# The planner of a hybrid encoder kernel gets other estimates of the waits of VectorE and GpSimd for their shared SBUF ports

## The chip, the cores and the metric

The kernel runs on one core of a Trainium2 chip. The metric is the device time of one execution in microseconds. TensorE (PE in the profile, its weight loads PEld), VectorE (DVE), ScalarE (ACT), GpSimd (POOL) and the DMA queue of SyncE (SP) each work through a list of instructions of their own, in a fixed order; semaphores tie the lists together.

## The reference: what is computed

Two sequences of 512 and 256 tokens with 1024 channels go through the same two layers. Each layer adds its mixer's output to the scaled input and normalises the sum over the channels:

```python
alpha = (2.0 * DEPTH) ** 0.25
for i in range(DEPTH):              # DEPTH = 2: kind 0, then kind 1
    if kind == 0:   h = _mamba2_mixer(x, ...)
    elif kind == 1: h = _rwkv7_mixer(x, ...)
    x = _layernorm(alpha * x + h, ln_g[i], ln_b[i])
```

The first mixer is a bidirectional Mamba-2 block: a projection to z, x, B, C and dt, a centred convolution of width 5 with a silu, a state-space scan in chunks of 128 tokens forward and backward, a gate with silu(z), an RMS norm in 8 groups, and a projection back. The second is a bidirectional RWKV-7 block: a projection to r, k, v, g and two low-rank inputs, a token shift, a decay and a learning rate for each channel, a delta-rule scan with a 64 x 64 state for each of 16 heads in both directions, a group norm, a bonus term, a gate and a projection back. All of it is float32.

## The kernel before, in words

The 768 tokens of both sequences are treated together. Every large projection is split: a float32 operand is rounded to a `float32r` part (ScalarE, L126, L139) and a rest (VectorE `tensor_sub`, L127, or for two of the eight input blocks GpSimd, L140), and three matmuls (L144 to L146) replace one.

The Mamba stage (about 0 to 620 us) loops over 8 channel groups. For each it projects four blocks, convolves them on VectorE (L236, L238, L244), builds for each of 6 chunks the weighted decay matrix `G` (GpSimd L418, VectorE L413, L419, L420) and the output `yv` (GpSimd L429 and L440, VectorE L441 and L442). The scale `sk` of the skip term is a small VectorE operation on 4 elements for each partition (L428) that reads two small SBUF tiles. The output projection and the layer norm follow until about 740 us.

The RWKV stage (about 840 to 1500 us) loops over 8 blocks of 128 channels. It projects r, k, v, g for a later block, prepares keys and decays in windows of 256 tokens (`p1_front`, `p1_back`: VectorE L880, L900, L906, L916, L919; GpSimd L903, L905, L907, L932, L934), inverts small triangular matrices (`rwkv_inverse`, L954 to L990), and runs the scan in 8 steps a block (`chain_step`: matmuls L1018 and L1040, GpSimd L1054, VectorE L1057, L1066, L1068). `rwkv_final` (L1091 to L1120) normalises the output, on GpSimd except in the last block. `rsqrt` (L100 to L112) is a chain of nine small VectorE operations, used by the RMS norm (`rms`), the key norm (`nk`), the group norm (`ng`) and the layer norm (`ln`). The output projection (L505) and the last layer norm end the program.

The order in which each engine issues its instructions is not that of the source. After the program is built, `arrange` (L1888) makes a model of it, plans it, and pins each engine's order with dependencies from each instruction to the one before it. Tiles and buffers are given out before that and do not depend on the plan. The model has a `cost` for each instruction (`estimate`, L1374), a table of times from one engine to the next (`HANDOVER`, L1248), and a model of TensorE's clock: a period in which too little dense matmul work was done is followed by one at half rate (`TICK`, `WARM`, L1859 on). `schedule` (L1811) builds 12 plans one after another for each of four parameter sets, each with due times from the plan before, and keeps the one with the best modelled time over four modelled runs, three of them with random DMA delays.

For the ports that VectorE and GpSimd share, an instruction may have a `lock`, the part of its cost during which it is taken to hold the ports. `Machine.run` uses it so:

```python
end = t + p.cost[i]
if p.lock[i]:
    other = "Pool" if e == "DVE" else "DVE"
    end = max(end, self.held[other] + p.lock[i])
    self.held[e] = end
```

An instruction with a lock thus cannot end earlier than `lock` after the end of the other engine's last locked instruction: `lock` is what remains to be done once the other engine lets go. In the kernel before, `lock` is `cost - 60` ns for every GpSimd operation but memsets, and for VectorE operations without a PSUM operand if they have more than 16 elements for each partition.

Of the kernel before, what the change touches and what calls it, by code (L numbers as in the profile page):

```python
# [59 lines left out]
class Trunk:  # L60
# [1103 lines left out]
    def run(self):  # L1164
        self.mamba()
        self.rwkv()
# [108 lines left out]
def size(ap, first=1):  # L1275
    return math.prod(int(n) for _, n in ap.ap[first:])


def on_chip(ap):

    (ps, pn), *free = [(int(s), int(n)) for s, n in ap.ap]
    p0, lo = divmod(int(ap.offset), ps) if ps else (0, int(ap.offset))
    bits = 1
    for k, (s, n) in enumerate(free):
        if n == 1 or s == 0:
            continue
        if k == len(free) - 1 and abs(s) > 1:
            s, n = int(math.copysign(1, s)), (n - 1) * abs(s) + 1
        if s < 0:
            lo += s * (n - 1)  # L1290
            s = -s
        cur, have, pos, acc = bits, 1, 0, 0
        while have <= n:
            if n & have:
                acc |= cur << (s * pos)
                pos += have
            cur |= cur << (s * have)
            have *= 2
        bits = acc
    return p0 // 32, (p0 + pn + 31) // 32, bits << lo  # L1300
# [19 lines left out]
def space(t, name):  # L1320
    return str(t._space).endswith(name)


class Program:
# [49 lines left out]
    def estimate(self, i, x, src, dst):  # L1374
        e, op = self.eng[i], x.opcode
        if e == "SP":
            dram = src and dst and any(hasattr(a.tensor, "cap_key") and space(a.tensor, "DRAM") for a in src + dst)
            self.cost[i] = 1.0 if not dst else 560.0 if dram else 400.0
            if dram and len(dst[0].ap) > 2:
                self.cost[i] = 650.0  # L1380
            if dst:
                n = size(dst[0], 0)
                self.dma[i] = n * 4 / 250.0
                self.late[i] = max(0, n / min(run(a) for a in src + dst) - 128) * 2.3
                if any(s == 0 and k > 1 for a in src for s, k in a.ap):
                    self.late[i] += 1100.0
            return
        if e == "PE":
            N, M, K = size(src[0]), size(src[1]), int(src[0].ap[0][1])
            f32 = str(x.ins[0].dtype) == "dt.float32"  # L1390
            up = lambda n: 32 if n <= 32 else 64 if n <= 64 else 128
            rows, cols = (range(*on_chip(a)[:2]) for a in (src[1], dst[0]))
            self.cells[i] = [4 * r + c for r in rows for c in cols]
            if x.is_transpose:
                self.cost[i] = 2 * max(N, M) / 2.4 + 2.5
                self.cols[i] = 2 * N * K / 128
                self.extra[i] = 57.0
                return
            self.mode[i] = up(K), up(M)
            if not f32:  # L1400
                r = self.fast[i] = str(x.ins[0].dtype) == "dt.float32r"
                self.extra[i] = 106.0
                self.cost[i] = (N * 17 / 16 + 16) / 2.4 if r else N / 2.4 + 2.0
                self.cols[i] = N * K / 128
                if N >= 256:
                    self.kind[i] = 2
                    if r and M <= 64:
                        self.mode[i] = FULL
                return
            cyc = 4 * max(N, M)  # L1410
            if M > 64 and N < 64:
                cyc = 1022
            self.cost[i] = cyc / 2.4 + 2.5
            self.cols[i] = (2 if M <= 64 else 4) * N * K / 128
            if M <= 64:
                self.cost[i], self.extra[i] = (114.5, 20.0) if max(K, M) <= 32 else (116.6 if N <= 64 else N * 1.703, 49.0)
                self.leave[i] = 100 + 0.82 * N
                self.kind[i] = 0
            return
        N = max(size(a) for a in src + dst)  # L1420
        rows = on_chip(dst[0])[:2] if hasattr(dst[0].tensor, "_space") and int(dst[0].ap[0][1]) > 1 else (0, 4)
        if rows != (0, 4) and int(dst[0].ap[0][1]) >= 32:
            self.part[i] = rows
        ps = any(space(a.tensor, "PSUM") for a in src + dst if hasattr(a.tensor, "_space"))
        ptr = sum(1 for a in src if size(a) == 1 and N > 1)
        two = len(src) - ptr
        if e == "DVE":
            if op != "TensorScalarPtr":
                c = (66 + N) / 0.96
                if op == "Reciprocal":  # L1430
                    c = 70 + N * 6.4
            elif x.ins and two == 1 and not ps:
                c = 69 + N / 1.92 + 61 * ptr
            else:
                c = (66 + N) / 0.96 + 61 * ptr
            if any(N > 64 and len(a.ap) > 1 and abs(int(a.ap[-1][0])) >= 16 and space(a.tensor, "SBUF") for a in src + dst):
                c += 0.78 * N
            if getattr(x, "is_tensor_tensor_scan", False):
                c = 70 + 2.07 * N
            if not ps and N > 16:  # L1440
                self.lock[i] = c - 60
        elif e == "Activation":
            far = any(N > 64 and len(a.ap) > 1 and abs(int(a.ap[-1][0])) >= 16 for a in src + dst)
            c = 51 + N * (1.9 if far else 0.8333) + (0 if ps else 43) + 93.5 * ptr + (93 if len(dst) > 1 else 0)
        elif op == "Memset":
            c = 35 + 0.8333 * N
        elif op == "TensorScalarPtr":
            c = 130 + N * 0.83 + 90 * ptr
            self.lock[i] = c - 60
        elif two > 1:  # L1450
            c = 185 + 1.6 * N if N < 200 else 222 + 1.75 * N
            self.lock[i] = c - 60
        else:
            c = 130 + 0.9 * N
            self.lock[i] = c - 60
        self.cost[i] = c

    def node(self, pred):
# [472 lines left out]
```

## Time and profile before

| what | before |
| --- | --- |
| time, median of 3 runs | 1620.61 us (1617.91 to 1621.78) |
| profiled execution, own time | 1633.23 us |
| span of the profiled execution | 1631.4 us |
| mean granted TensorE clock | 0.955 |
| instructions | 39329 |
| PE busy | 1516.9 us (93%) |
| VectorE busy | 1342.4 us (82%) |
| ScalarE busy | 858.0 us (53%) |
| GpSimd busy | 709.8 us (44%) |

The profile is one execution. A group's row names the line, the engine, the operation, the tiles it writes and reads, the shape and the count, then the busy time in us, the mean duration of one in ns, and the engine's idle time before the group with what ended it. A row for one line gives the least, the median and the largest duration in ns. The time that an operation waits for the ports is inside its duration, since it has started by then.

### The profile page before, as it was taken

What the parts mean: (1) busy time and instruction counts of PE and PEld (TensorE: products, weight loads), DVE (VectorE), ACT (ScalarE), POOL (GpSimd) and SP (SyncE); (2) the same over time, 40 slices, a digit from 0 to 9 for tenths busy, and PEclk for the clock granted to TensorE, in tenths of its full rate; (3) what the DMA queues carried; (4) which work ended last, traced back from release to release, by engine and by line L of the source; (5) the groups of instructions that cost most, each with busy time, mean ns of one, the idle gap of its engine ahead of it and who ended that gap; (6) DMA issues with size and microseconds to landing.
All of it is one profiled execution on the core that took longest, in us unless ns stands there. A gap on an engine that the chain in (4) does not pass through costs nothing. (4 is left out here: it accounts for less than half of the span.)

```text
span 1631.4 us, 39329 instructions
## 1 busy us (share of the span) xinstructions
PE 1516.9 (93%) x15210; PEld 1287.0 (79%) x15210; DVE 1342.4 (82%) x2947; ACT 858.0 (53%) x1988; POOL 709.8 (44%) x983
## 2 busy tenths in 40 slices
PE   7999999999999899998987899989998989978996
PEld 6878888888889699997766777777777777766876
DVE  6769988898797995668689798889899897887759
ACT  4245454544444452424464758577675747574332
POOL 1158475585483670000162527355464628264210
PEclk9999999999999999999989899989999999986988
DMA  5110211212212044612345234443435242344422
GB/s 171 58 52 21 79 39 59 72 65 72 66 40 72 23 154 122 196 53 104 119 128 157 54 116 118 119 141 104 140 99 159 82 140 83 105 145 135 139 71 85
DMA packets 150315, 161.41 MB, mean 99 GB/s; under 512 B 39632, under 2 KB 106928, under 8 KB 150128
## 3 DMA queue, kind: packets, MB, share of 16 engines
q1 hardware_dynamic: 150128, 158.89, 32.2%
q8 instruction: 120, 1.97, 0.5%
q14 instruction: 67, 0.55, 0.1%
HBM read 121.43 MB, written 40.55 MB: 99 GB/s over the span
## 5 line engine op out<-in xcount | busy, mean ns | idle before, releaser
L144 PE MATMUL pj<-xh,whi 128*128 128x512 f32 (+1 forms) x1056 | 381.6, 361 | 20.4 <-ACT whi L126 11.6
L146 PE MATMUL pj<-xh,wlo 128*128 128x256 f32 (+1 forms) x1056 | 374.8, 355 | 3.9 <-DVE wlo L127 3.9
L145 PE MATMUL pj<-xl,whi 128*128 128x512 f32 (+1 forms) x1056 | 373.7, 354 | 0.9 <-DVE xl L140 0.9
L144 PEld LDWEIGHTS pj<-xh,whi 128*128 128x128 f32 x1056 | 205.2, 194 | 50.9 <-ACT whi L126 13.0
L146 PEld LDWEIGHTS pj<-xh,wlo 128*128 128x128 f32 x1056 | 204.2, 193 | 30.6 <-DVE wlo L127 6.4
L145 PEld LDWEIGHTS pj<-xl,whi 128*128 128x128 f32 x1056 | 204.6, 194 | 25.8 <-issue 2.1
L126 ACT CAST whi<-wraw 128x512 fp32r<-128x512 f32 x213 | 131.1, 620 | 128.2 <-PE pj L145 57.9
L127 DVE TENSOR_TENSOR wlo<-wraw,whi 128x512 fp32r<-128x512 f32 x213 | 156.1, 738 | 40.2 <-ACT whi L126 38.1
L418 POOL TENSOR_SCALAR G<-past,ddt,dt 128x128 f32<-128x128 f32 x192 | 133.6, 708 | 73.7 <-DVE ddt L324 59.0
L144 PE MATMUL po<-whi,xh 128*128 128x256 f32 x528 | 153.0, 290 | 0.6 <-DVE acc L505 0.5
L145 PE MATMUL po<-wlo,xh 128*128 128x256 f32 x528 | 152.9, 290 | 0.0
L146 PE MATMUL po<-whi,xl 128*128 128x256 f32 x528 | 152.2, 288 | 0.0
L238 DVE SCALAR_TENSOR_TENSOR conv<-conv,convw 128x770 f32<-128x770 f32 x128 | 142.2, 1111 | 1.4
L144 PE MATMUL pz<-whi,xh 128*128 128x256 f32 x384 | 114.7, 299 | 0.0
L382 POOL TENSOR_TENSOR xw<-xB,dtws 128x256 f32<-128x256 f32 x64 | 55.7, 877 | 130.7 <-ACT xB L370 115.3
L145 PE MATMUL pz<-wlo,xh 128*128 128x256 f32 x384 | 111.9, 291 | 0.0
L146 PE MATMUL pz<-whi,xl 128*128 128x256 f32 x384 | 110.2, 287 | 0.0
L903 POOL TENSOR_TENSOR G<-EP,Wr 64x256 f32<-64x256 f32 x96 | 85.5, 891 | 49.4 <-DMA Wr<-ind 26.9
L1054 POOL TENSOR_TENSOR ZP<-SV,PC 64x128 f32<-64x128 f32 x128 | 68.4, 543 | 86.2 <-DVE SV L1066 59.8
L144 PEld LDWEIGHTS po<-whi,xh 128*128 128x128 f32 x528 | 101.7, 193 | 2.3 <-DVE acc L505 0.9
L145 PEld LDWEIGHTS po<-wlo,xh 128*128 128x128 f32 x528 | 102.2, 194 | 1.6 <-DVE wlo L127 0.6
L146 PEld LDWEIGHTS po<-whi,xl 128*128 128x128 f32 x528 | 102.0, 193 | 1.2
(289 smaller groups left out, 3831.4 us busy)
## 6 DMA issues: line engine op xcount, KB each, us to landing
wraw<-in_r_w_in SPq DMA_DIRECT2D x72, 256.0 KB, 3.1
Wr<-ind SPq DMA_DIRECT2D x48, 384.0 KB, 3.7
wraw<-in_m_w_xbc SPq DMA_DIRECT2D x64, 256.0 KB, 2.6
wraw<-in_m_w_z SPq DMA_DIRECT2D x32, 256.0 KB, 2.7
wraw<-in_m_w_out SPq DMA_DIRECT2D x32, 256.0 KB, 3.0
ydram<-yst SPq DMA_DIRECT2D x16, 384.0 KB, 4.6
yraw<-ydram SPq DMA_DIRECT2D x24, 256.0 KB, 4.9
ind<-k SPq DMA_DIRECT2D x32, 192.0 KB, 2.8
```

The source lines that it names most:

```text
L126: nc.scalar.copy(hi, raw)
L127: nc.vector.tensor_sub(lo, raw, hi.bitcast(F32))
L144: mm(ps, ah, bh, start=first, stop=False)
L145: mm(ps, ah, bl, start=False, stop=False)
L146: mm(ps, al, bh, start=False, stop=last)
L238: nc.vector.scalar_tensor_tensor(acc, u[:, t : t + n], w[:, b, t : t + 1], acc, op0=ALU.mult, op1=ALU.add)
L382: nc.gpsimd.tensor_tensor(hv(xw), hv(xB[c][:, 0:256]), bc(self.dtws[:, c, z, hs], 2, 64), op=ALU.mult)
L418: nc.gpsimd.tensor_scalar(G[:, h, :], self.past, self.ddt[:, c, i : i + 1], self.dt[:, c, 0, i : i + 1], op0=ALU.mult, op1=ALU.add)
L903: nc.gpsimd.tensor_tensor(G[hr, ps4, h, 0, :], EP[hr, :, 0:C], w4(tok(W[hr, h])), op=ALU.mult)
L1054: nc.gpsimd.tensor_tensor(ZP[HR[h], :, s, :], SV[HR[h], :, s, h, :], bc(pc[s][HR[h]], 2, C), op=ALU.mult)
```

## The change

Only `estimate` is changed, and only `lock`, with one `cost`. For VectorE operations without a PSUM operand the lock becomes `cost - 52`, and operations of 16 elements or fewer get one too. For GpSimd the lock becomes `cost - 95` (operations with scalars from SBUF, `TensorScalarPtr`), `cost - 130` (two tensor inputs) or `cost - 87` (the rest). A GpSimd operation on two tensors whose output is `float32r` costs 115 ns more. The instructions, their operands, the tiles and their places stay as they are; the plan is made anew with these numbers, so the order may differ on every engine and in SyncE's queue.

```diff
-            if not ps and N > 16:
-                self.lock[i] = c - 60
+            if not ps:
+                self.lock[i] = c - 52
...
         elif op == "TensorScalarPtr":
             c = 130 + N * 0.83 + 90 * ptr
-            self.lock[i] = c - 60
+            self.lock[i] = c - 95
         elif two > 1:
             c = 185 + 1.6 * N if N < 200 else 222 + 1.75 * N
-            self.lock[i] = c - 60
+            if str(x.outs[0].dtype) == "dt.float32r":
+                c += 115
+            self.lock[i] = c - 130
         else:
             c = 130 + 0.9 * N
-            self.lock[i] = c - 60
+            self.lock[i] = c - 87
         self.cost[i] = c
```

## The prediction, made before the result was known

> **What bounds the kernel now.** I read the page first, then the busy time by stretches, then who TensorE waited for, then the groups of VectorE and GpSimd in the stretch that has slack. The page:
>
> ```profile
> span 1631.4 us, 39329 instructions
> PE 1516.9 (93%) x15210; PEld 1287.0 (79%) x15210; DVE 1342.4 (82%) x2947; ACT 858.0 (53%) x1988; POOL 709.8 (44%) x983
> ```
>
> TensorE is the bound, with 1631.4 - 1516.9 = 114.5 us idle. The stretches (start and end, length, busy us of PE, PEld, DVE, ACT, POOL with instruction counts, granted clock, DMA share, GB/s) say where; the row of sums is that of six stretches from 20 to 620 us:
>
> ```profile
> sum 600.00, PE 590.50 PEld 510.86 DVE 512.64 ACT 283.13 POOL 334.60; mean PE 98.42 PEld 85.14 DVE 85.44 ACT 47.19 POOL 55.77
> ...
> 840.00:1500.00 660.00, 596.97 (x7939) 475.85 (x7939) 578.22 (x1310) 425.50 (x1047) 327.14 (x491) 0.92 0.41 119
> ...
> 1150.00:1250.00 100.00, 92.27 (x1181) 72.51 (x1180) 91.40 (x220) 62.28 (x154) 49.63 (x72) 0.97 0.44 127
> ...
> 1400.00:1450.00 50.00, 43.76 (x539) 35.11 (x539) 46.10 (x125) 30.73 (x72) 20.03 (x28) 0.89 0.50 147
> 1450.00:1500.00 50.00, 40.45 (x598) 32.72 (x597) 40.47 (x79) 33.24 (x89) 30.85 (x48) 0.77 0.42 122
> ```
>
> In the Mamba stage PE is busy 590.5 of 600 us: whatever VectorE and GpSimd do there lies under matmuls. In the RWKV stage (840 to 1500) PE is idle 660 - 597 = 63 us, its clock is 0.92, and VectorE is busy 578 of 660 (0.88): the two share the bound. Who PE waited for, over the whole span (total us, times, longest):
>
> ```profile
> PE pf L1105 <- POOL Y L1101: 16.5, 7, 3.5
> PE pj L144 <- ACT whi L126: 11.6, 2, 11.2
> ...
> PE ptd L914 <- POOL G L905: 3.4, 4, 2.3
> ```
>
> GpSimd is named for 16.5 + 3.4 = 19.9 us, all of it in or behind the RWKV stage.
>
> **The change part by part.** It removes and adds no instruction and no DMA: 39329 stay 39329. Every effect comes through the order. So I ask first whether the new numbers are nearer to the trace, then what a better plan can be worth.
>
> *How near.* When one engine holds the ports, the other's operation ends a fixed time after the holder's. Four contests in order of time (start us, duration us, engine, line):
>
> ```profile
> 148.66 0.73 POOL L440 TENSOR_TENSOR yv<-yv,yo 128x256 f32<-128x256 f32 x1
> ...
> 148.74 0.70 DVE L428 SCALAR_TENSOR_TENSOR sk<-dt,ss,dskip 128x4 f32<-128x4 f32 x1
> 149.36 0.68 DVE L127 TENSOR_TENSOR wlo<-wraw,whi 128x512 fp32r<-128x512 f32 x1
> ...
> 149.38 0.98 POOL L418 TENSOR_SCALAR G<-past,ddt,dt 128x128 f32<-128x128 f32 x1
> ```
>
> ```profile
> 810.30 1.06 DVE L906 TENSOR_TENSOR KB<-KB,ld 128x512 f32<-128x512 f32 x1
> 811.29 1.17 DVE L900 TENSOR_TENSOR KB<-KB,Wr 128x512 f32<-128x512 f32 x1
> ...
> 810.77 1.14 POOL L905 TENSOR_TENSOR G<-EP,Wr 64x256 f32<-64x256 f32 x1
> ```
>
> L905 ends at 811.91, 0.55 us after L906 (811.36). Its cost in the plan is 222 + 1.75 x 256 = 670 ns, so the old lock is 610, the new 540. L418 ends at 150.36, 0.32 after L127 (150.04); cost 130 + 0.83 x 128 + 180 = 416, old 356, new 321. L900 ends at 812.46, 0.55 after L905; cost (66 + 512)/0.96 = 602, old 542, new 550. L428, 4 elements wide, ends at 149.44, 0.05 after L440 (149.39); the old plan has no wait and ends it 134 ns after its start, at 148.87; the new lock is 82 ns, which gives 149.47. All four move towards the trace: GpSimd's wait was planned 35 to 70 ns too long, a small VectorE operation's not at all.
>
> *Where it can count.* Groups of the stretch 840 to 1500 us, and behind them least, median and largest duration of the same lines over the whole span:
>
> ```profile
> L905 POOL TENSOR_TENSOR G<-EP,Wr 64x256 f32<-64x256 f32 x85 | 80.2, 944 | 1.2
> L903 POOL TENSOR_TENSOR G<-EP,Wr 64x256 f32<-64x256 f32 x85 | 74.5, 876 | 36.1 <-DMA Wr<-ind 26.9 <-PE pr L1018 4.1
> L1054 POOL TENSOR_TENSOR ZP<-SV,PC 64x128 f32<-64x128 f32 x112 | 61.7, 559 | 55.3 <-DVE SV L1066 33.7 <-DVE SV L1068 17.8
> ...
> L127 DVE TENSOR_TENSOR wlo<-wraw,whi 128x512 fp32r<-128x512 f32 x57 | 43.2, 758 | 5.6 <-ACT whi L126 5.1
> L900 DVE TENSOR_TENSOR KB<-KB,Wr 128x512 f32<-128x512 f32 x42 | 38.3, 913 | 2.1 <-ACT KB L899 1.6
> L906 DVE TENSOR_TENSOR KB<-KB,ld 128x512 f32<-128x512 f32 x43 | 38.1, 888 | 0.4
> L880 DVE TENSOR_TENSOR_SCAN ld<-scanm,ld 128x256 f32<-128x256 bf16 x42 | 33.4, 795 | 1.4 <-ACT ld L879 1.1
> ```
>
> ```profile
> L905 POOL TENSOR_TENSOR G<-EP,Wr x96: 669/863/3039, 810.8 to 1477.6; 64x256 f32<-64x256 f32 x96
> L1054 POOL TENSOR_TENSOR ZP<-SV,PC x128: 392/402/1297, 910.2 to 1578.7; 64x128 f32<-64x128 f32 x128
> L127 DVE TENSOR_TENSOR wlo<-wraw,whi x213: 657/685/1905, 11.2 to 1580.5; 128x512 fp32r<-128x512 f32 x107
> L900 DVE TENSOR_TENSOR KB<-KB,Wr x48: 649/849/1230, 809.6 to 1474.2; 128x512 f32<-128x512 f32 x48
> L906 DVE TENSOR_TENSOR KB<-KB,ld x48: 652/826/1173, 810.3 to 1475.9; 128x512 f32<-128x512 f32 x48
> L880 DVE TENSOR_TENSOR_SCAN ld<-scanm,ld x48: 641/691/1233, 792.4 to 1465.0; 128x256 f32<-128x256 bf16 x48
> ```
>
> Mean less least, times count, is time in port waits. VectorE: L127 5.8, L900 11.1, L906 10.1, L880 6.5, together 33.5 us of 578. GpSimd: L905 (944 - 669) x 85 = 23.4, L903 by L905's least 17.6, L1054 18.7, together 59.7 us. A held L905 above waited 1.14 - 0.67 = 0.47 us, so about 59.7/0.47 = 127 GpSimd operations are held (an estimate); each was planned 70 ns too long, 8.9 us in the stage.
>
> *The sum.* That 8.9 us is the drift between planned and real GpSimd that the change takes out. A drifted GpSimd operation meets a VectorE operation that it was planned to miss. The worth of this isn't in the trace; I bound it. Below: nothing, since GpSimd is busy only 327 of 660 us. Above: half of VectorE's 33.5 us, 17 us, since GpSimd has the ports half of the stage in any order. I take the value nearest to the drift: 8.9 x 0.88 (VectorE's load) x 0.90 (PE's, 597 of 660) = 7.1 us. The other edits come to nothing. The small operations:
>
> ```profile
> L428 DVE SCALAR_TENSOR_TENSOR sk<-dt,ss,dskip x48: 205/220/702, 128.3 to 617.7; 128x4 f32<-128x4 f32 x48
> ```
>
> L428 lies in the Mamba stage under PE; without that cover one long wait costs 702 - 205 = 0.5 us. Its mean wait can't be more than half of that, so the whole edit stays below 48 x 0.25 = 12 us of VectorE time, all of it in a stage that PE fills. The 115 ns concern two splits on GpSimd in the first 20 us, 0.23 us under the 11.2 us for which PE waits for its first weights (L126); uncovered they cost those 0.23. Every engine's order and SyncE's issues move with the plan too; I cost that at 0, bounded by the 26.9 us for which L903 waited for `Wr`, all on GpSimd.
>
> Sum: 1633.23 - 7.1 = 1626.1 us for a profiled execution. The runs stand to it as 1620.61/1633.23 = 0.9923, so **1614 us**.
>
> A rule of the Trainium skill speaks against a large gain: SBUF — State Buffer, section "Who interferes with whom", says that the issue order and not the shape decides who blocks, and that the loser waits for the whole of the other's instruction. The contests above agree (L900 took 1.17 us against its least of 0.65). By that rule a contest called wrongly costs a whole L905, 669 ns, and not the 70 ns of the estimate's error, in either direction.
>
> **The rivals.** *No difference.* The plan is tied at every step to semaphores, and 70 ns fades at the next one; the order changes, the time doesn't: 1620.6 us, within 0.3% (1615.7 to 1625.5), which is about what a measurement of this kernel can tell from no change. For it: GpSimd has half the stage free, and the old VectorE lock of 542 was right already. Against it: small changes of a cost reorder a list plan widely.
>
> *Slower, through TensorE's clock.* A new order shifts dense projections against the sparse scan steps; where PE falls behind, its clock falls too. In 1150 to 1250, busy time times clock is 92.27 x 0.97 = 89.5; in 1400 to 1500 it is 43.76 x 0.89 + 40.45 x 0.77 = 70.1. Another 100 us like the latter costs 19.4 us, half of one 10 to 12: 1632. It decides once some 50 us more of the RWKV stage drop below 0.9 of the clock. For it: the stage is near that edge already at 0.92; against it, the plan models the clock, and that part is untouched.
>
> *Slower, through small operations.* GpSimd work now kept clear of the `rsqrt` chains is put off, and `Y` (L1101), which PE already awaits 16.5 us, comes later; 7 times 0.67 us (one L905 each) and as much again in the scan, about 8 us: 1627.
>
> *A larger gain.* The new order happens to fill 1400 to 1500: 19.4 us less of lost work, 1602. The same dice as in the first slower case, on the other side.
>
> **How the numbers follow.** Forecast (1606 to 1617) 0.33, of which 0.04 falls within 0.3%; no difference 0.25; clock 0.25; small operations 0.05; larger gain 0.12. Faster 0.29 + 0.12 = 0.41, same 0.29, slower 0.30. The range, 1600 to 1636, reaches to both clock cases, and leaves out about 0.1. The forecast's own range is 1606 to 1617.
>
> **What would show it.** Right: the means of L900, L906 and L880 in the RWKV stage fall, together by some 7 us, L905 and L903 fall below 944 and 876 ns, L428 keeps few waits, and the clock of the stage stays at 0.92. Wrong: port waits of the same 33.5 us with an end that moved with the granted clock or with PE's idle time; then the order's chance decided, not the estimates. A Mamba stage that changes by more than 3 us would show that its cover was thinner than I read it.

## The result, and the profile after

The changed kernel takes 1605.43 us (median of 4 runs, 1600.35 to 1607.35), the kernel before beside it 1619.26 us (median of 4 runs, of which three gave the 1620.61 above): a ratio of 0.9899 with a 95% interval of 0.9861 to 0.9937. That is 1.0% faster, about two and a half times the forecast's 0.4%, and inside the stated range. One execution in all the runs of this document lies apart: of nine of the changed kernel with VectorE's 1 ns (below) one took 4577.23 us, and it is in no ratio.

The two profiled executions lie further apart than the medians: 1600.35 against 1633.23 us, and the one of before is not typical of its kernel. In three later sets of runs that kernel's median was 1615.8 to 1617.4 us, and none of its 49 executions there took more than 1626.65 us. Their mean granted clocks were 0.960 to 0.972, 0.967 in the mean; the profiled one's 0.955 lies below all of them. What the two traces show is therefore the direction, some 33 us of it, of which about 14 is the change.

The page of the changed kernel, as quoted of before:

```profile
span 1598.5 us, 39340 instructions
...
PE 1497.7 (94%) x15210; PEld 1266.0 (79%) x15210; DVE 1340.6 (84%) x2947; ACT 857.1 (54%) x1988; POOL 712.0 (45%) x983
```

Seen from TensorE, the 32.9 us of span are two parts: its idle time goes from 114.5 to 1598.5 - 1497.7 = 100.8 us (13.7 less), and its busy time from 1516.9 to 1497.7 us (19.2 less) for the same 15210 matmuls. The second part goes with a clock that was granted more of the time: 0.955 in this execution of before, now

```profile
core 0: 1598.5 us, clock 0.978
```

The four executions of the changed kernel had 0.973 to 0.980. So between the kernels the clock rose from about 0.967 to about 0.977, and the other half of the step from 0.955 is that one execution of before.

The 11 instructions more (39340 for 39329) are semaphore waits that another order needs, none of them work; the prediction had put the count as unchanged. GpSimd's busy time, which holds its port waits, rose from 709.8 to 712.0 us. The stretches show where TensorE gained; the second to fourth row have the same bounds as before, the first is the sum of six stretches from 20 to 620 us:

```profile
sum 600.00, PE 591.27 PEld 508.62 DVE 509.46 ACT 284.46 POOL 332.09; mean PE 98.54 PEld 84.77 DVE 84.91 ACT 47.41 POOL 55.35
```

```profile
840.00:1500.00 660.00, 611.33 (x8195) 486.67 (x8194) 599.53 (x1370) 431.09 (x1065) 335.47 (x492) 0.97 0.44 125
...
1400.00:1450.00 50.00, 42.84 (x639) 35.74 (x639) 45.71 (x97) 33.29 (x80) 29.47 (x38) 0.90 0.48 139
1450.00:1500.00 50.00, 42.46 (x545) 35.39 (x544) 47.32 (x112) 23.35 (x62) 22.85 (x32) 0.93 0.46 135
```

The Mamba stage stayed as it was (591.3 of 600 us against 590.5). The RWKV stage even begins a little later: the first L900, which prepares its keys, starts at 811.4 us, 809.6 before.

```profile
L900 DVE TENSOR_TENSOR KB<-KB,Wr x48: 656/793/1196, 811.4 to 1456.2; 128x512 f32<-128x512 f32 x48
```

So the whole gain lies behind that point. In the RWKV stage TensorE issued 8195 matmuls and transposes in the same 660 us, against 7939, at a clock of 0.97 against 0.92. The last 50 us of it, 0.77 before, are at 0.93.

What of the port waits? The groups of the same stretch in the changed kernel:

```profile
L127 DVE TENSOR_TENSOR wlo<-wraw,whi 128x512 fp32r<-128x512 f32 x63 | 48.1, 764 | 2.7 <-ACT whi L126 2.4
L900 DVE TENSOR_TENSOR KB<-KB,Wr 128x512 f32<-128x512 f32 x42 | 37.2, 886 | 5.5 <-DMA Wr<-ind 3.7 <-ACT KB L899 1.2
L906 DVE TENSOR_TENSOR KB<-KB,ld 128x512 f32<-128x512 f32 x42 | 35.9, 856 | 0.4
L880 DVE TENSOR_TENSOR_SCAN ld<-scanm,ld 128x256 f32<-128x256 bf16 x42 | 31.9, 759 | 1.8 <-ACT ld L879 1.2
```

```profile
L903 POOL TENSOR_TENSOR G<-EP,Wr 64x256 f32<-64x256 f32 x84 | 78.8, 938 | 36.9 <-DMA Wr<-ind 30.5 <-PE pr L1018 1.7
L905 POOL TENSOR_TENSOR G<-EP,Wr 64x256 f32<-64x256 f32 x84 | 78.1, 929 | 2.5 <-PE py L1040 1.5
L1054 POOL TENSOR_TENSOR ZP<-SV,PC 64x128 f32<-64x128 f32 x112 | 58.3, 529 | 36.8 <-DVE SV L1066 29.3 <-DVE SV L1068 3.3
```

On VectorE the means moved from 913, 888, 795 and 758 ns (L900, L906, L880, L127) to 886, 856, 759 and 764. For the counts of before that is 27 x 42 + 32 x 43 + 36 x 42 - 6 x 57 = 3.7 us less waiting. On GpSimd L905 and L1054 wait a little less (944 to 929 and 559 to 529 ns) and L903 more (876 to 938): 62 x 85 - 15 x 85 - 30 x 112 ns, together 0.6 us more. So the waits that the change is about hardly moved.

Who TensorE waited for, after:

```profile
PE pf L1105 <- POOL Y L1101: 14.6, 7, 3.2
PE pj L144 <- ACT whi L126: 11.7, 2, 11.3
PE ptd L914 <- DVE G L919: 7.9, 8, 1.9
...
PE ptd L914 <- POOL G L905: 2.7, 5, 1.0
```

In these rows GpSimd is named for 17.3 us, 19.9 before (shorter rows add 1.4 us after and 0.9 before). For the `G` of VectorE (L919) TensorE waits longer, 7.9 us against 2.8.

### The profile page after: what moved, and what is told of

The parts are those of the page before. It is cut to its first block, busy times and chain, and to the rows that moved or that the text cites. A ratio compares the mean times of both kernels' runs of the same rounds, so it can differ in the third digit from the quotient of the medians.

```text
span 1598.5 us, 39340 instructions
## 1 busy us (share of the span) xinstructions
PE 1497.7 (94%) x15210; PEld 1266.0 (79%) x15210; DVE 1340.6 (84%) x2947; ACT 857.1 (54%) x1988; POOL 712.0 (45%) x983
## 4 chain that ended last, share of the span: by engine, by line
PE 67%; DVE 16%; POOL 6%; DMA 4%; issue 3%; ACT 3%; SPq 0%; DVEq 0%; POOLq 0%; ACTq 0%
PE pj L144 9%; PE pj L145 9%; PE pj L146 9%; PE pz L146 3%; PE pz L145 3%; PE pz L144 3%; PE po L146 3%; PE po L145 3%; PE po L144 3%; PE py L1040 2%; PE ptd L914 2%; PE pst L384 2%; PE py L423 2%; DVE tl L965 2%; DVE XN L964 2%
## 5 line engine op out<-in xcount | busy, mean ns | idle before, releaser
L146 PE MATMUL pj<-xh,wlo 128*128 128x512 f32 (+1 forms) x1056 | 375.0, 356 | 1.6 <-DVE wlo L127 1.6
L127 DVE TENSOR_TENSOR wlo<-wraw,whi 128x512 fp32r<-128x512 f32 x213 | 157.9, 747 | 34.5 <-ACT whi L126 33.5
L418 POOL TENSOR_SCALAR G<-past,ddt,dt 128x128 f32<-128x128 f32 x192 | 136.0, 720 | 94.4 <-DVE ddt L324 59.2
L903 POOL TENSOR_TENSOR G<-EP,Wr 64x256 f32<-64x256 f32 x96 | 88.2, 919 | 51.2 <-DMA Wr<-ind 30.5
L1054 POOL TENSOR_TENSOR ZP<-SV,PC 64x128 f32<-64x128 f32 x128 | 64.9, 515 | 59.4 <-DVE SV L1066 48.4
```

What stands on the lines that cost most here:

```text
L127: nc.vector.tensor_sub(lo, raw, hi.bitcast(F32))
L146: mm(ps, al, bh, start=False, stop=last)
L418: nc.gpsimd.tensor_scalar(G[:, h, :], self.past, self.ddt[:, c, i : i + 1], self.dt[:, c, 0, i : i + 1], op0=ALU.mult, op1=ALU.add)
L903: nc.gpsimd.tensor_tensor(G[hr, ps4, h, 0, :], EP[hr, :, 0:C], w4(tok(W[hr, h])), op=ALU.mult)
L1054: nc.gpsimd.tensor_tensor(ZP[HR[h], :, s, :], SV[HR[h], :, s, h, :], bc(pc[s][HR[h]], 2, C), op=ALU.mult)
```

## The experiments

Two theories stood against each other. The theory of the estimates: numbers nearer to the trace give an order with fewer or cheaper port waits, and that is the gain. The theory of the draw: any small change of any estimate deals another order, and the time scatters with it. Each ratio below is to the kernel before in runs beside it on the same chip, with its 95% interval.

### The change in parts, and a change that has nothing to do with ports

GpSimd's locks alone:

```diff
         elif op == "TensorScalarPtr":
-            self.lock[i] = c - 60
+            self.lock[i] = c - 95
         elif two > 1:
-            self.lock[i] = c - 60
+            self.lock[i] = c - 130
         else:
-            self.lock[i] = c - 60
+            self.lock[i] = c - 87
```

> Only GpSimd's three lock formulas are changed (cost - 95, - 130, - 87); VectorE's lock and the cost of float32r outputs stay as before. Theory of the estimates: this is where the plan was furthest from the trace (35 to 70 ns for each held operation), so most of the gain is here: 1605 to 1612 us, with VectorE's port waits in the RWKV stage below those of before. Theory of the draw (any small change of the estimates deals a new order, and the time scatters with it): anywhere from 1603 to 1630, with no tie to the port waits, but with one to the granted clock.

VectorE's 8 ns alone:

```diff
             if not ps and N > 16:
-                self.lock[i] = c - 60
+                self.lock[i] = c - 52
```

> Only VectorE's lock is changed, cost - 52 for cost - 60, 8 ns, and still none for 16 elements or fewer. Theory of the estimates: 8 ns of 550 are nothing, 1616 to 1622 us. Theory of the draw: 8 ns are enough for a new order; 1603 to 1630.

The small operations alone:

```diff
-            if not ps and N > 16:
+            if not ps:
                 self.lock[i] = c - 60
```

> Only the small VectorE operations get a lock (cost - 60, like the larger ones of before). Theory of the estimates: they lie in the Mamba stage under TensorE, so 1616 to 1622 us, with the mean of L428 lower than 304 ns. Theory of the draw: 1603 to 1630, whatever L428 does.

SyncE's issue:

```diff
-            self.cost[i] = 1.0 if not dst else 560.0 if dram else 400.0
+            self.cost[i] = 1.0 if not dst else 562.0 if dram else 400.0
```

> A change that has nothing to do with ports: on the kernel before, SyncE's issue of a plain DMA is taken as 562 ns and not 560. Theory of the estimates: no difference, within 0.3% of the kernel before. Theory of the draw: a new order, and a time off by up to 10 us to either side.

Measured: GpSimd's locks 1.0034 (1.0008 to 1.0060), 1624.7 us; VectorE's 8 ns 0.9930 (0.9899 to 0.9961), 1606.9 us; the small operations 1.0045 (1.0025 to 1.0065), 1625.2 us; SyncE's 2 ns 0.9942 (0.9912 to 0.9972), 1607.9 us. The kernel before took 1615.8 us beside them.

The part that corrects the largest error makes the kernel slower by itself, the 8 ns that should be nothing make it 0.7% faster, and 2 ns on SyncE, which has no part in the locks, make it 0.6% faster. The small operations alone are slower, and the wait that they were to take from L428 didn't go. The group's row of the kernel before, and then of this one:

```profile
L428 DVE SCALAR_TENSOR_TENSOR sk<-dt,ss,dskip 128x4 f32<-128x4 f32 x48 | 14.5, 304 | 0.2
```

```profile
L428 DVE SCALAR_TENSOR_TENSOR sk<-dt,ss,dskip 128x4 f32<-128x4 f32 x48 | 15.0, 312 | 0.3
```

The mean is 304 ns before and 312 here. The first of these kernels also shows that port waits and time can move against each other. Its page (GpSimd's locks alone):

```profile
PE 1511.3 (93%) x15210; PEld 1279.6 (79%) x15210; DVE 1342.3 (83%) x2947; ACT 857.5 (53%) x1988; POOL 696.5 (43%) x983
```

GpSimd's 983 operations take 696.5 us, 13.3 less than before and 15.5 less than in the changed kernel, and yet at 1624.7 us it is 19 us slower than the changed one.

### More draws, on both kernels, and the wrong direction

```diff
-    "DVE": {"PE": 135, "DVE": 112, "Activation": 113, "Pool": 145, "SP": 110},
+    "DVE": {"PE": 135, "DVE": 113, "Activation": 113, "Pool": 145, "SP": 110},
```

On the kernel before:

> Another change that has nothing to do with ports, on the kernel before: VectorE's time to itself across a true dependency is taken as 113 ns and not 112. Theory of the estimates: no difference from the kernel before. Theory of the draw: another order; 1603 to 1626 us, as far from before as the four parts tried so far (0.7% faster to 0.5% slower).

On the changed kernel, first SyncE's 2 ns of above, then this 1 ns:

> The change as it is, and SyncE's issue of a plain DMA taken as 562 ns and not 560. Theory of the estimates: the ports are still described better, so it stays at the changed kernel's time, 1600 to 1610 us. Theory of the draw: the changed kernel's 1605 was one draw; this is another, 1603 to 1626, and more likely slower than 1605 than not.

> The change as it is, and VectorE's time to itself taken as 113 ns and not 112. Theory of the estimates: 1600 to 1610 us. Theory of the draw: 1603 to 1626.

GpSimd's locks moved the other way, in the kernel before:

```diff
         elif op == "TensorScalarPtr":
-            self.lock[i] = c - 60
+            self.lock[i] = c - 25
         elif two > 1:
-            self.lock[i] = c - 60
+            self.lock[i] = c + 10
         else:
-            self.lock[i] = c - 60
+            self.lock[i] = c - 33
```

> GpSimd's locks are moved by as much the other way: cost - 25 with scalars from SBUF, cost + 10 with two tensors, cost - 33 for the rest; VectorE as before. A held GpSimd operation is then planned 70 to 140 ns too long. Theory of the estimates: slower than before by as much as the change is faster, 1625 to 1640 us. Theory of the draw: 1603 to 1630, no worse than the right direction (1625).

Measured: the kernel before with 1 ns 0.9955 (0.9939 to 0.9972), 1611.6 us; the changed kernel with SyncE's 2 ns 1.0033 (1.0017 to 1.0050), 1624.1 us; the changed kernel with 1 ns 1.0030 (1.0014 to 1.0045), 1621.8 us; the wrong direction 1.0046 (1.0031 to 1.0061), 1624.7 us.

This is the clearest answer: 2 ns on SyncE take the changed kernel from 0.9899 to 1.0033, and the better estimates of the ports are still in it. And the right direction for GpSimd's locks alone (1.0034) is no better than the wrong one (1.0046) beyond their intervals. VectorE's waits are the same in the changed kernel and in that with SyncE's 2 ns, whose rows are

```profile
L127 DVE TENSOR_TENSOR wlo<-wraw,whi 128x512 fp32r<-128x512 f32 x58 | 43.9, 759 | 4.2 <-ACT whi L126 2.9 <-PE pj L146 0.3 <-issue 0.2
L906 DVE TENSOR_TENSOR KB<-KB,ld 128x512 f32<-128x512 f32 x45 | 39.9, 889 | 0.4
L900 DVE TENSOR_TENSOR KB<-KB,Wr 128x512 f32<-128x512 f32 x44 | 38.1, 867 | 4.3 <-ACT KB L899 3.0 <-DMA Wr<-ind 0.6
L880 DVE TENSOR_TENSOR_SCAN ld<-scanm,ld 128x256 f32<-128x256 bf16 x44 | 33.2, 756 | 3.0 <-ACT ld L879 2.6
```

Against the changed kernel's means that is, for 42 of each and 57 of L127, 1.4 - 0.8 - 0.1 - 0.3 = 0.2 us more. The difference begins before that stretch. The first L900 of the kernel with SyncE's 2 ns:

```profile
L900 DVE TENSOR_TENSOR KB<-KB,Wr x48: 656/694/1206, 824.9 to 1479.6; 128x512 f32<-128x512 f32 x48
```

It starts at 824.9 us, 13.5 us later than in the changed kernel. The two traces' spans differ by 23.7 us (1622.2 and 1598.5), so more than half of that is lost ahead of the RWKV stage: from 20 to 620 us TensorE is busy 582.6 us with SyncE's 2 ns and 591.3 in the changed kernel. The other 10 us or so are lost behind it, at a clock of 0.94 from 840 to 1500 us, not 0.97.

### What port waits are worth at a fixed order

Here the order itself was held: GpSimd's products in L903 and L905 are filled with a constant (the result is meaningless), while the plan goes on treating them as products, so that every engine's list stays that of the kernel before.

```diff
-            nc.gpsimd.tensor_tensor(G[hr, ps4, h, 0, :], EP[hr, :, 0:C], w4(tok(W[hr, h])), op=ALU.mult)
+            self.fill(G[hr, ps4, h, 0, :], EP[hr, :, 0:C], w4(tok(W[hr, h])))
...
-            nc.gpsimd.tensor_tensor(rho[..., ::-1] if z else rho, EP[hr, :, 1:], w4(tok(W[hr, 2])), op=ALU.mult)
+            self.fill(rho, EP[hr, :, 1:], w4(tok(W[hr, 2])))
...
+    def fill(self, out, *src):
+        self.planned[self.nc.gpsimd.memset(out, 1e-24).ins.name] = list(src), [out]
...
+            if x.name in planned:
+                io = list(planned[x.name])
+                x = Product(x)
```

> The order of every engine is exactly that of the kernel before, instruction for instruction. Left out: the 192 products of GpSimd in L903 and L905; in their place GpSimd fills the same places of G with a constant, which reads nothing, so the numbers behind G mean nothing. The waits of VectorE for these operations go (of the 33.5 us in the RWKV stage the larger part, L900, L906 and L880) and GpSimd is done earlier. If VectorE's port waits lie on the path, as the prediction's sum has it, the time falls by 0.8 of what VectorE no longer waits, 15 to 25 us. If they lie in slack, it stays within 5 us of the kernel before.

Measured: 0.9947 (0.9930 to 0.9964), 1609.8 us against 1617.2. VectorE's groups of 840 to 1500 us:

```profile
L127 DVE TENSOR_TENSOR wlo<-wraw,whi 128x512 fp32r<-128x512 f32 x58 | 40.3, 695 | 4.1 <-ACT whi L126 3.6
L880 DVE TENSOR_TENSOR_SCAN ld<-scanm,ld 128x256 f32<-128x256 bf16 x42 | 30.6, 729 | 4.8 <-ACT ld L879 4.5
L906 DVE TENSOR_TENSOR KB<-KB,ld 128x512 f32<-128x512 f32 x43 | 30.5, 711 | 0.4
L900 DVE TENSOR_TENSOR KB<-KB,Wr 128x512 f32<-128x512 f32 x42 | 29.5, 704 | 4.8 <-ACT KB L899 2.3 <-DMA Wr<-ind 1.8
```

VectorE waits (758 - 695) x 57 + (795 - 729) x 42 + (888 - 711) x 43 + (913 - 704) x 42 = 22.8 us less, and the time falls by 0.0053 x 1617.2 = 8.6 us (5.8 to 11.3 by the interval): 0.38 us for each us of waiting, 0.50 at the interval's end. That is under half of the 18.2 us that the sum's factor of 0.8 gives for 22.8, and more than the 5 us of slack. GpSimd is also done earlier here (its busy time in this run is 593 us), and that is in the same 8.6 us, so a VectorE wait alone is hardly worth more than that. A change of the clock through the constant data does not show: the six executions had 0.964 to 0.971, the kernel before beside them 0.964 to 0.970. At 0.38 the changed kernel's 3.7 us less waiting are worth 1.4 us of its 14 to 16, at 0.50 under 2.

### A plan that knows nothing of the ports, and two more

All locks zero:

```diff
-                self.lock[i] = c - 60
+                self.lock[i] = 0.0
...
-            self.lock[i] = c - 60
+            self.lock[i] = 0.0
```

> The plan knows nothing of the shared ports: all locks are zero. Theory of the estimates: the worst of all, slower than before by more than the change is faster, over 1635 us, with more port waits. Theory of the draw: 1603 to 1630, like any other small change of the estimates.

Measured: 1.0311 (1.0271 to 1.0351), 1669.5 us. This one lies outside the scatter of the others: three times as far from the kernel before as any of them. TensorE's waits, the first 620 us and the first L900 of it:

```profile
PE ptd L914 <- POOL G L905: 17.6, 19, 2.9
```

```profile
0.00:620.00 620.00, 580.54 (x4044) 491.81 (x4045) 495.62 (x920) 280.63 (x603) 311.53 (x403) 1.00 0.21 66
```

```profile
L900 DVE TENSOR_TENSOR KB<-KB,Wr x48: 658/838/1241, 840.5 to 1514.2; 128x512 f32<-128x512 f32 x48
```

The same stretch of the kernel before:

```profile
0.00:620.00 620.00, 598.99 (x4298) 518.14 (x4299) 522.53 (x976) 294.33 (x632) 339.78 (x429) 0.99 0.23 72
```

More than half of the loss lies in the Mamba stage, where the prediction had seen nothing to gain or lose. TensorE is idle 39 us in the first 620, 21 before, and the first L900 starts at 840.5 us, 30.9 later than in the kernel before (809.6). The medians differ by 52 us. In the RWKV stage TensorE waits 17.6 us for GpSimd's `G` in L905, 3.4 before. The port waits do not explain this by their sum: VectorE is busy 1353.2 us, 10.8 more, and GpSimd 696.2, 13.6 less, while TensorE is idle 1660.7 - 1509.8 = 150.9 us, 36.4 more. What this plan lost is the cover, the matmuls that TensorE can run while the other engines wait for each other. In this one order a plan that knows nothing of the ports is 3% slower; whether it has their lock right to 70 ns is lost in the scatter of the orders.

The change without its 115 ns for float32r outputs:

```diff
             if str(x.outs[0].dtype) == "dt.float32r":
-                c += 115
+                c += 0
```

> The change without its 115 ns for a float32r output, which touches two GpSimd operations in the first 20 us. Theory of the estimates: the changed kernel's time, 1600 to 1610 us. Theory of the draw: 1603 to 1626.

Measured: 0.9901 (0.9874 to 0.9929), 1603.1 us. Its order is on every engine the changed kernel's, instruction for instruction, so this part of the change does nothing, and the run is a second measurement of the changed order in another set of runs. It gives the same 1.0%: the time belongs to the order, and is repeatable.

The clock's threshold in the plan, on the kernel before:

```diff
-WARM = 2900
+WARM = 3200
```

> The ports as in the kernel before; the plan believes that TensorE's clock needs 3200 columns of dense work in a period and not 2900, so it spreads that work with more margin. If the time goes with the clock, and the plan can steer it, the mean granted clock rises to 0.975 or more and the time falls to 1600 to 1610 us, like the changed kernel's. If orders are draws in this too: 1603 to 1630.

Measured: 1.0064 (1.0039 to 1.0088), 1627.7 us, and a granted clock of

```profile
core 0: 1628.6 us, clock 0.963
```

against the 0.975 that was expected; the eight executions had 0.958 to 0.965, none above the mean of before. Asking the plan for more margin did not buy the clock.

### What goes with the time

From the pages, for the ten kernels that differ from before by small estimates alone (the changed one and its second run among them) and for before itself, in the order of the profiled span; idle is the span less PE's busy time:

| kernel | span | PE idle | mean clock | GpSimd busy | first L900 starts |
| --- | --- | --- | --- | --- | --- |
| changed | 1598.5 | 100.8 | 0.978 | 712.0 | 811.4 |
| changed, no 115 ns (same order) | 1601.2 | 104.5 | 0.980 | 713.2 | 814.5 |
| before, SyncE 2 ns | 1607.0 | 104.7 | 0.966 | 717.0 | 812.2 |
| before, VectorE 1 ns | 1610.7 | 110.3 | 0.962 | 702.0 | 816.8 |
| VectorE's lock | 1613.9 | 112.4 | 0.964 | 703.3 | 813.4 |
| changed, VectorE 1 ns | 1619.2 | 113.9 | 0.966 | 695.3 | 816.8 |
| changed, SyncE 2 ns | 1622.2 | 115.2 | 0.968 | 700.0 | 824.9 |
| GpSimd's locks, wrong way | 1622.2 | 117.6 | 0.958 | 692.9 | 813.6 |
| GpSimd's locks | 1622.8 | 111.5 | 0.964 | 696.5 | 814.9 |
| small operations | 1623.2 | 116.2 | 0.956 | 698.5 | 816.6 |
| before | 1631.4 | 114.5 | 0.955 | 709.8 | 809.6 |

The span goes with TensorE's idle time. With the granted clock it goes only at the ends: the changed order has the highest clock in both of its rows, and in the rows from 1607 to 1623 us there is little order in the clocks. The means over all executions say the same: 0.967 for the kernel before and for GpSimd's locks, which are slower, 0.966 for VectorE's lock, which is faster, 0.969 for the changed kernel with SyncE's 2 ns, which is slower. The kernel before is last here by its one profiled execution; by the medians it lies in the middle.

GpSimd's busy time, which would be low if fewer port waits made a kernel fast, is lower in the slow ones if anything. The last column says where a kernel fell behind. The changed order comes to its first L900 no earlier than before, at 811 and 815 us in its two rows, and then takes 787 us to the end in both, the least of all; the changed kernel with SyncE's 2 ns is last at that point. This is a table of what goes together. Which placement in an order sets the idle time and the clock, and which of the two comes first, no run here tells: the one attempt to move the clock by itself failed.

## Why the prediction was right, and where it was not

**The time and the sign.** 1605 lies in the range of 1600 to 1636, and faster had the largest chance. It lies just outside the forecast's own range (1606 to 1617), next to the case called a larger gain (1602, "the same dice as in the first slower case, on the other side"). That case, which had 0.12, is nearer to what happened than the forecast's mechanism. That 1605 lies in the range is mostly luck: the range was wide for the sake of other cases, and the mechanism that was priced gave about 1.4 of some 14 us.

By the prediction's own signs the result is split. The means of L900, L906 and L880 fell, but by 4.0 us together and not 7; L905 fell below 944 ns, and L903 rose above 876; the clock of the stage did not stay at 0.92. An end that moves with clock and idle time was its sign that the order's chance decided.

**How near the new numbers are.** That the locks of four contests move towards the trace stands: it was read from the rows, and nothing after spoke against it. The plan's errors there were 60 ns for L905 (610 planned, 0.55 us in the trace) and 36 ns for L418, where the locks moved by 70 and 35: L905's new lock of 540 ns is about 10 too short.

**What they are worth.** This is the step that failed, in two places. First the term "8.9 us of drift, taken out by the change": VectorE's waits fell by 3.7 us and GpSimd's busy time rose; the drift did not come back as fewer waits. Second the factor 0.88 x 0.90 with which waiting was turned into time: at a fixed order it is about 0.38, and 0.50 at the end of the interval. Together 1.4 us, or under 2, and not 7.1. The other 12 us of the gain go with another order's idle time and clock, which 2 ns on SyncE undo. The prediction did cost a new order, at 0, and that is the term that mattered.

**The edits costed at nothing.** The 115 ns are nothing exactly: the order is the same without them. The small operations have no part in the gain that can be shown: alone they are 0.45% slower, and L428's mean of 304 ns only fell to 279 in the changed kernel,

```profile
L428 DVE SCALAR_TENSOR_TENSOR sk<-dt,ss,dskip 128x4 f32<-128x4 f32 x48 | 13.3, 279 | 0.3
```

1.2 us in all, in the stage that TensorE fills. As a rival they were wrong too: `Y` (L1101) isn't awaited longer, 14.6 us against 16.5. That they are slower in their own kernel says as little as the other draws. The rival's price was also added up wrong: 7 x 0.67 us and as much again is 9.4 us, not 8, which is 1630 us and not 1627. In the same way the larger gain's 1620.6 - 19.4 is 1601, not 1602.

**No difference.** Its argument, that 70 ns fade at the next semaphore, is refuted: even 1 or 2 ns change the order on all engines and move the time by 0.4 to 1.3%.

**The clock.** It was listed as the way in which the time could go to either side, at 19.4 us for 100 us like those from 1400 to 1500. In the changed kernel these are 42.84 x 0.90 + 42.46 x 0.93 = 78.0 of work, against 70.1, 8 us more at the same times, though not of quite the same work; the rest is spread over the stage. The condition was right in kind. One outcome cannot show that its chance of 0.12 on the good side was too small beside the forecast's 0.33; that edits of no meaning moved the time by 0.4 to 1.3% suggests it.

**The cover in the Mamba stage** held in the changed kernel: less than 1 us of change in 600, as written, and 1.8 us at the first L900. But it belongs to the order and not to the stage. With SyncE's 2 ns the same change reaches the first L900 13.5 us later, and the plan without locks 30.9 us later than before. That whatever VectorE and GpSimd do there lies under matmuls was true of the orders that had been looked at, no more.

The rule of the Trainium skill that was weighed there (SBUF — State Buffer, "Who interferes with whom": the issue order decides who blocks, and the loser waits out the whole instruction) agrees with the contests shown there. The plan without locks adds nothing to it: L905's mean from 840 to 1500 us is 936 ns there and 944 before, so its contests cost no more each; what grew is how long TensorE waits for the product, 17.6 us instead of 3.4.

**What stays open.** Whether the better locks have a mean effect below what single draws show: with them three orders gave 0.990, 1.003 and 1.003, with the old ones 1, 0.994 and 0.996. That is no sign of a gain, and too few to exclude 0.5%. And which property of the changed order gives TensorE its idle time back: the gain is put down to the order because the same order repeats it and edits without meaning undo it, not because the placement that does it was found.

No run beat the changed kernel: its order, at 1603 to 1605 us, is the fastest of all that ran with the full computation, though the intervals of VectorE's 8 ns (0.9899 to 0.9961) and of SyncE's 2 ns (0.9912 to 0.9972) overlap with its own (0.9861 to 0.9937).

## What to carry to other kernels

Where an order comes from a list planner, an edit of its estimates is a new draw first and a better model second: time a few edits that should do nothing (1 or 2 ns somewhere) before a gain of 1% is put down to the edit's idea. Correcting a model paid where it was blind (3% here, in one order, for ports that it knew nothing of) and not, as far as these runs can see, where it is off by tens of nanoseconds. What lies under other work in one order need not in the next, so a stage that looks covered is compared again with each plan. An order that turned out well can be kept as it is; here the same order gave its 1.0% again in other runs.

## What the runs showed of the hardware

Two sources of lost time that the forecast had not priced against each other: about 23 us of VectorE's port waits taken away at a fixed order gave 8.6 us, while the profiled execution with a granted clock of 0.978 had 19.2 us less of TensorE's busy time for the same matmuls than the one with 0.955. About half of that step in the clock lies between executions of one kernel: 49 of the kernel before had 0.960 to 0.972. And the spread of good and bad orders of one program, from small edits of the estimates, was 1.5% of its time (0.9899 to 1.0046).
